# A gated recurrence beside full matmuls: products moved from GpSimd to VectorE, two scalings from VectorE to ScalarE

## The chip, the cores and the metric

The kernel runs on one core of one Trainium2 chip. The metric is the device time of one execution in microseconds, as the median of a few runs. The core has TensorE (PE, matmuls), VectorE (DVE), ScalarE (ACT), GpSimd (POOL) and SyncE (SP, which here only issues DMAs). Each engine works through its own instructions in a fixed order and waits where one of them needs a result of another engine.

## The reference, cut to what matters

One layer on 1024 prompt rows and 64 sample rows, 1024 wide (T = 1088 rows in all). The input is normed and projected; the columns of the projection are the recurrent branch's path `xa` and gate `ga`, the attention's q, k, v, and gates. Then, for the recurrent branch:

```python
ua, conv_new = causal_conv(xa, conv_hist, conv_w, conv_b)          # 4 taps: b + sum full[tap:tap+L] * w[tap]
r = sigmoid(einsum(ub, w_a) + b_a); i = sigmoid(einsum(ub, w_x) + b_x)
log_a = -LRU_C * r * softplus(-a_param)
a = exp(log_a); x_in = sqrt(-expm1(2 * log_a)) * (i * u)
h_t = a_t * h_{t-1} + x_t                                          # scan over the rows
ya = h * silu(ga)
```

Attention with forgetting runs beside it; both branches are projected, merged by sigmoid gates, projected again, normed and added.

## The kernel before, in words

The matmuls of this kernel reach fp32 precision by three passes: each operand is split into a high part (a copy on ScalarE, `wh`, `uh`, `yah`) and a low part (the difference on VectorE, `wl`, `ul`, `yal`), and `three` multiplies high by high, low by high and high by low. A weight panel is 1024 x 128; a panel against all rows takes 72 matmuls in three chunks of some 364 rows. `panel()` hands out a panel that is already split and at once splits the next one (ScalarE `wh`, L82, then VectorE `wl`, L85), into one of two buffers.

The stages are: norm and values (v); q, k and a few other panels by seven products of half-sized blocks for eight (`seven`, up to about 420 us), which `put` (L750) writes to DRAM; attention, with leftover panels between; the recurrence (about 862 to 1082 us); the two branch projections; the output projections.

In the products of halves `put` gets each half of a result from PSUM. Kind "r" (x's first panel, and the gate panels 1, 3 and 5 named by `GA_EARLY`) is stored as it is: a ScalarE copy or a VectorE add, and a DMA. The orders of ScalarE and VectorE are free in that stage.

In the recurrence the orders of TensorE, ScalarE and VectorE are the program's (L1466 and the manual schedule around it). Channels come in eight panels of 128, k = 0 to 7, and a tile holds 1092 columns: 1024 prompt rows, three of padding, 64 sample rows, and one more. Even and odd k have a set of tiles each (odd ones have names with `_e`), and each tile exists once, so the next even channel must wait until the last even one has been read. The steps for one k:

- `recur_in` (L1300): the gate weights' DMA, x's panel by TensorE, copied out by ScalarE into `xp`, one copy a chunk.
- `convolve` (L1332): the gate weights split (`g_h` on ScalarE, `g_l` on GpSimd), the first tap with its bias (L1339, VectorE), three more taps (L1342, VectorE) into `u`.
- `split_u` (L1346), `gate` (L1354): 18 matmuls, six sigmoids on ScalarE into `x` and `r`, then x times u (L1364) on GpSimd.
- `decay` (L1367): Exp and Tanh on ScalarE. `decay_a` (L1376): q, then 1-q (L1380), on VectorE. `root` (L1387): square root on ScalarE.
- `state_in` (L1391): two products on VectorE and one column copied by GpSimd. `scan` (L1398): VectorE's scan.
- `output` (L1410): the state times the gate's silu (L1420, L1421) on GpSimd, written over `sg` for even k. `split_y` (L1423): `yah`, `yal`.
- `own_gate` (L1428): the gate's panel, its sigmoid on ScalarE and product on VectorE chunk by chunk; for k = 1, 3, 5 a load of the stored panel, whose silu `early_gate` (L1443) takes in two instructions.

The loop (L1473) takes two channels a pass, k = 0, 2, 4, and a tail (L1512) the last two. Within a pass the steps of four channels are interleaved: `gate(k)` and `own_gate(k)`, `state` and `output` of k-1, x's panel of k+2, `gate(k+1)`, `convolve(k+2)`, then both decays, x's panel of k+3, both roots, `state(k)`. PSUM has eight banks in this stage.

Of the kernel before, what the change touches and what calls it, by code (L numbers as in the profile page):

```python
# [7 lines left out]
F32 = mybir.dt.float32  # L8
F32R = mybir.dt.float32r
AF = mybir.ActivationFunctionType  # L10
ALU = mybir.AluOpType
AX = mybir.AxisListType

P = 128
D = 1024
KT = D // P
SEQ = 1024
DEC = 64
T = SEQ + DEC
# [12 lines left out]
HT = T // 2  # L32
# [4 lines left out]
W_SC = 1092  # L37
# [28 lines left out]
def hybrid_step(tc, a, o):  # L66
    nc = tc.nc
    PSUM = bass.MemoryType.PSUM
    act, dve, pool, pe, sp = nc.scalar, nc.vector, nc.gpsimd, nc.tensor, nc.sync
# [8 lines left out]
    def f(ap):  # L78
        return ap.bitcast(F32)
# [4 lines left out]
    def sub(eng, out, in0, in1):  # L84
        return eng.tensor_tensor(out=out, in0=in0, in1=in1, op=ALU.subtract)  # L85
# [11 lines left out]
    d_x0 = dram.tile([P, T], F32, name="d_x0")  # L97
# [119 lines left out]
    quads = [([cols(c + p * P)], ((t, p), (t, p + 1))) for p in range(0, NP, 2) for c, t in ((C_K, "k"), (C_Q, "q"))]  # L217
    some = [(cols(C_XA, 1), d_x0)] + [(cols(C_GA + k * P, 1), d_ga[k]) for k in GA_EARLY]
    for (s1, d1), (s2, d2) in (some[:2], some[2:]):
        quads.append(([s1, s2], (("r", d1), ("r", d2))))  # L220
    for _ in range(MORE):
        src, (d1, d2) = gates.pop()
        quads.append(([src], (("r", d1), ("r", d2))))
# [387 lines left out]
    sp_ = sb("quad")  # L611
# [138 lines left out]
    def put(kind, arg, z, in1, h):  # L750

        s = kqp.tile([P, HT], F32, name="ko", tag="ko", bufs=4)
        s3 = s.rearrange("p (c n) -> p c n", c=2)
        if in1 is None:
            copy_act(s3, z)
        else:
            dve.tensor_tensor(out=s3, in0=z, in1=in1, op=ALU.add)
        if kind == "r":
            (act if in1 is None else sp).dma_start(arg[:, h * HT:(h + 1) * HT], s[:, :])
            return  # L760
        d = d_k if kind == "k" else d_q
        h_ = slice(h * HT, (h + 1) * HT)
        hi = sp_.tile([P, HT], F32R, name="oh", tag="oh", bufs=2)
        scale = 1.0 if kind == "k" else HD ** -0.5
        copy_act(hi[:, :], s[:, :], scale)
        act.dma_start(d[0, arg][:, h_], f(hi[:, :]))
        lo = sp_.tile([P, HT], F32, name="kl", tag="kl", bufs=1) if kind == "k" else s
        dve.scalar_tensor_tensor(out=lo[:, :], in0=s[:, :], scalar=scale, in1=f(hi[:, :]),
                                 op0=ALU.mult, op1=ALU.subtract)
        sp.dma_start(d[1, arg][:, h_], lo[:, :])  # L770
        if kind == "k":
            kept[arg, h] = s
            p = arg - arg % 2
            if (p, h) in kept and (p + 1, h) in kept:
                ss = [kept.pop((p + j, h)) for j in range(2)]
                c = 0
                for blocks in ((P, P), (P, P), (HT - 4 * P,)) if h == 0 else ((P, P), (P, SEQ - HT - 3 * P), (DEC,)):
                    owed.append((n_prod[0] + 1, lambda c=c, blocks=blocks: keys_out(p, ss, c, h * HT + c, blocks)))
                    c += sum(blocks)
# [510 lines left out]
    def cv(v, k):  # L1290
        return vt[:, v + k:v + k + 1]
# [3 lines left out]
    def room(name, k):  # L1295
        if k in lent_k:
            return lent[name][:, :]
        return p3.tile([P, T if name == "sg" else W_SC], F32, name=name)[:, :]
# [33 lines left out]
    def convolve(k):  # L1332
        xp, raw, gh, gl = xps.pop(k)
        copy_act(gh[:, :, :], raw[:, :, :])
        sub(pool, gl[:, :, :], raw[:, :, :], f(gh[:, :, :]))
        pool.tensor_copy(fin[:, 0:3, k], xp[:, SEQ:SEQ + 3])
        pool.tensor_copy(fin[:, 3:6, k], xp[:, W_SC - 1:W_SC + 2])
        u = room("u", k)
        dve.tensor_scalar(out=u, in0=xp[:, 0:W_SC], scalar1=cv(V_CW, k), scalar2=cv(V_CB, k),  # L1339
                          op0=ALU.mult, op1=ALU.add)  # L1340
        for tap in range(1, 4):
            dve.scalar_tensor_tensor(out=u, in0=xp[:, tap:tap + W_SC], scalar=cv(V_CW + tap * KT, k),  # L1342
                                     in1=u, op0=ALU.mult, op1=ALU.add)
        us[k], gws[k] = u, (gh, gl)
# [9 lines left out]
    def gate(k):  # L1354

        (u, uh, ul), (gh, gl) = us.pop(k), gws.pop(k)
        x, r = room("x", k), room("r", k)
        for i, dst, bias in ((1, x, V_BX), (0, r, V_BA)):
            for c in range(3):
                cs_ = slice(c * GC, (c + 1) * GC)  # L1360
                acc = mm.tile([P, 512], F32, name="gacc", tag="acc")
                three(acc[:, :GC], gh[:, i, :], gl[:, i, :], uh[:, cs_], ul[:, cs_], True, True)
                act.activation(out=dst[:, cs_], in_=acc[:, :GC], func=AF.Sigmoid, bias=cv(bias, k))
        (dve if k == KT - 1 else pool).tensor_tensor(out=x, in0=x, in1=u, op=ALU.mult)  # L1364
        sig[k] = x, r

    def decay(k):  # L1367

        x, r = sig[k]
        col = slice(k, k + 1)  # L1370
        e = room("e", k)
        act.activation(out=e, in_=r, func=AF.Exp, scale=nsp8[:, col])
        act.activation(out=r, in_=r, func=AF.Tanh, scale=sp4[:, col])
        eq[k] = e

    def decay_a(k):  # L1376
        e, t = eq[k], sig[k][1]
        q = room("q", k)
        dve.scalar_tensor_tensor(out=q, in0=e, scalar=1.0, in1=t, op0=ALU.add, op1=ALU.mult)
        dve.tensor_scalar(out=q, in0=q, scalar1=-1.0, scalar2=1.0, op0=ALU.mult, op1=ALU.add)  # L1380
        pool.memset(q[:, SEQ:SEQ + 3], 0.0)
        eq[k] = e, q

# [7 lines left out]
    def state_in(k):  # L1391
        (x, r), (e, q) = sig[k], eq[k]
        dve.scalar_tensor_tensor(out=r, in0=e, scalar=1.0, in1=r, op0=ALU.add, op1=ALU.mult)
        dve.tensor_tensor(out=x, in0=x, in1=r, op=ALU.mult)

        pool.tensor_copy(x[:, SEQ + 2:SEQ + 3], cv(V_H0, k))

    def scan(k):  # L1398
        col = slice(k, k + 1)
# [10 lines left out]
    def output(k):  # L1410
        sg, (r, e) = silus.pop(k), states.pop(k)
        if k == 5:
            y = p3.tile([P, W_SC + 3], F32, name="xp")[:, :W_SC]
        elif k == 7:
            y = room("r", 0)
        else:
            y = r if k in lent_k else sg
        outs[k] = y
        eng = dve if k == KT - 1 else pool
        eng.tensor_tensor(out=y[:, :SEQ], in0=e[:, :SEQ], in1=sg[:, :SEQ], op=ALU.mult)  # L1420
        eng.tensor_tensor(out=y[:, SEQ:T], in0=e[:, SEQ + 3:SEQ + 3 + DEC], in1=sg[:, SEQ:T], op=ALU.mult)  # L1421

    def split_y(k):  # L1423
        y = outs.pop(k)[:, :T]
        copy_act(ya[k][0][:, :T], y)
        sub(dve, ya[k][1][:, :T], y, f(ya[k][0][:, :T]))

    def own_gate(k):  # L1428
        sg = silus[k] = room("sg", k)

        def evac(c, t0, n, z):
            c_ = slice(t0, t0 + n)
            act.activation(out=sg[:, c_], in_=z, func=AF.Sigmoid)
            dve.tensor_tensor(out=sg[:, c_], in0=z, in1=sg[:, c_], op=ALU.mult)

        if k in GA_EARLY:
            sp.dma_start(sg[:, :T], d_ga[k])
            return None
        tag, w = panel()
        assert tag == ("g", k)  # L1440
        return panel_steps(mm, *w, xs, evac)

    def early_gate(k):  # L1443
        sg = silus[k]
        s = room("q", 0)
        act.activation(out=s[:, :T], in_=sg, func=AF.Sigmoid)
        dve.tensor_tensor(out=sg, in0=s[:, :T], in1=sg, op=ALU.mult)

    class Held:

# [21 lines left out]
    run(xa)  # L1472
    for k in range(0, KT - 2, 2):  # L1473
        gate(k)
        convolve(k + 1)
        if k:
            early_gate(k - 1)
        ga = own_gate(k)
        if k:
            split_y(k - 2)  # L1480
        chunk(ga)
        split_u(k + 1)
        chunk(ga)
        if k:
            state(k - 1)
            output(k - 1)
        run(ga)
        own_gate(k + 1)
        xa = recur_in(k + 2)
        chunk(xa)  # L1490
        chunk(xa)
        if k:
            split_y(k - 1)
        run(xa)
        gate(k + 1)
        convolve(k + 2)
        decay(k)
        xa = recur_in(k + 3)
        split_u(k + 2)
        decay_a(k)  # L1500
        chunk(xa)
        decay(k + 1)
        decay_a(k + 1)
        chunk(xa)
        root(k)
        root(k + 1)
        set_sigmoid()
        state(k)
        output(k)
        run(xa)  # L1510

    k = KT - 2  # L1512
    gate(k)
    convolve(k + 1)
    split_y(k - 2)
    split_u(k + 1)
    ga = own_gate(k)
    chunk(ga)
    chunk(ga)
    state(k - 1)  # L1520
    run(ga)
    early_gate(k - 1)
    output(k - 1)
    gate(k + 1)
    ga = own_gate(k + 1)
    decay(k)
    decay_a(k)
# [53 lines left out]
    for of in range(KT):  # L1581
        g = g_next
# [324 lines left out]
```

## Time and profile before

| | us |
|---|---|
| median of 3 runs (1490.17 to 1494.55) | 1492.96 |
| the profiled execution | 1493.34 |
| its span, first to last instruction | 1491.4 |
| TensorE busy | 1451.8 (97%) |
| VectorE busy | 884.6 (59%) |
| ScalarE busy | 689.6 (46%) |
| GpSimd busy | 367.9 (25%) |

A busy share is a mean over all stages. In the profile's rows a tile's name stands with an arrow to what it was computed from, `L` gives the line of the code, and a bracket at the end of a row of the timeline says how long the engine had been idle before it and what it waited for. The mean granted clock of TensorE is 0.988 of full speed.

### The profile page before, as it was taken

The numbers are of one execution on the slowest core, as the hardware profiler recorded it, in microseconds if no ns is written. First come the engines' busy times: TensorE is split into PE (matmuls) and PEld (weight loads), VectorE is DVE, ScalarE is ACT, GpSimd is POOL, SyncE is SP. The second block draws the span as 40 slices with busy tenths as digits, with TensorE's granted clock in tenths as the row PEclk, the third lists the DMA queues.
The fourth block names the chain that finished last, engine by engine and source line by source line (L and its number), as shares of the span: only waits on it lengthen the run. The fifth ranks groups of instructions, "written<-read, shape, count | busy, mean of one in ns | idle before, by whom it ended". The sixth has DMA issues, their size and how long they took to land.

```text
span 1491.4 us, 26313 instructions
## 1 busy us (share of the span) xinstructions
PE 1451.8 (97%) x10096; PEld 1427.3 (96%) x10096; DVE 884.6 (59%) x1516; ACT 689.6 (46%) x1327; POOL 367.9 (25%) x443
## 2 busy tenths in 40 slices
PE   7999999999999999999999999989999999999997
PEld 7999999999999999999899999988999999999997
DVE  5464765664326666666556556999755545337644
ACT  4423444442225566565555536556544323334633
POOL 3012332322322333233233223555322000000001
PEclk9999999999999999999999999999999999999999
DMA  5367455753375756555753331211276544215111
GB/s 201 107 128 102 144 164 172 192 182 101 105 199 147 135 130 154 116 134 131 135 133 95 59 86 38 55 42 39 88 254 237 197 135 140 86 34 170 47 47 43
DMA packets 141081, 182.84 MB, mean 123 GB/s; under 512 B 23164, under 2 KB 111708, under 8 KB 140956
## 3 DMA queue, kind: packets, MB, share of 16 engines
q1 hardware_dynamic: 123292, 155.53, 40.2%
q10 hardware_dynamic: 17664, 25.64, 4.9%
q8 instruction: 79, 1.29, 0.3%
q14 instruction: 46, 0.38, 0.1%
HBM read 122.65 MB, written 58.46 MB: 121 GB/s over the span
## 4 chain that ended last, share of the span: by engine, by line
PE 80%; DVE 8%; ACT 5%; DMA 3%; issue 2%; POOL 1%; SPq 0%; ACTq 0%; DVEq 0%; POOLq 0%
PE quad L726 16%; PE acc L160 13%; PE acc L158 13%; PE acc L159 13%; PE tp L1068 4%; PE pv L1096 3%; PE pv L1098 2%; PE s L1046 2%; PE s L1047 2%; PE vacc L158 1%; PE vacc L159 1%; PE vacc L160 1%; DVE u L1342 1%; DMA out_v_prompt<-v_sb 1%; PE vacc L456 1%
## 5 line engine op out<-in xcount | busy, mean ns | idle before, releaser
L160 PE MATMUL acc<-xh,wl 128*128 128x364 f32 (+1 forms) x768 | 253.4, 330 | 6.8 <-DVE wl L85 6.8
L158 PE MATMUL acc<-xh,wh 128*128 128x364 f32 (+1 forms) x768 | 254.3, 331 | 0.4 <-ACT st L82 0.4
L159 PE MATMUL acc<-xl,wh 128*128 128x364 f32 (+1 forms) x768 | 253.0, 329 | 0.0
L160 PEld LDWEIGHTS acc<-xh,wl 128*128 128x128 f32 x768 | 145.5, 189 | 7.4 <-DVE wl L85 7.4
L158 PEld LDWEIGHTS acc<-xh,wh 128*128 128x128 f32 x768 | 146.0, 190 | 1.4 <-ACT st L82 0.7
L159 PEld LDWEIGHTS acc<-xl,wh 128*128 128x128 f32 x768 | 145.7, 190 | 0.6
L85 DVE TENSOR_TENSOR wl<-w_raw,wh 128x1024 fp32r<-128x1024 f32 (+1 forms) x66 | 84.7, 1285 | 56.5 <-ACT wh L82 55.6
L1031 POOL TENSOR_SCALAR pb<-pb,sm 128x896 f32<-128x896 f32 (+1 forms) x64 | 61.7, 964 | 203.5 <-DVE sm L1030 184.0
L1026 DVE CUSTOM_DVE_ANT_0 s<-s,mask 128x1024 f32<-128x1024 f32 (+7 forms) x128 | 95.4, 767 | 25.5 <-PE s L1047 25.2
L82 ACT ACTIVATE wh<-w_raw 128x1024 fp32r<-128x1024 f32 (+1 forms) x66 | 64.4, 977 | 60.9 <-PE quad L726 27.5
L85 DVE TENSOR_TENSOR tl<-tp,th 128x512 fp32r<-128x512 f32 x96 | 65.8, 689 | 36.9 <-ACT th L82 36.8
L726 PE MATMUL quad<-xh,wh 128*128 128x272 f32 x384 | 80.7, 291 | 0.0
L726 PE MATMUL quad<-xl,wh 128*128 128x272 f32 x384 | 79.5, 288 | 0.0
L726 PE MATMUL quad<-xh,wl 128*128 128x272 f32 x384 | 79.4, 288 | 0.0
L1028 ACT ACTIVATE pb<-s,nm 128x896 f32<-128x896 f32 (+1 forms) x64 | 61.2, 955 | 33.9 <-DVE nm L1026 25.0
L82 ACT ACTIVATE th<-tp 128x512 fp32r<-128x512 f32 x96 | 57.0, 597 | 41.0 <-PE tp L1068 37.0
L158 PE MATMUL acc<-wqh,hth 128*128 128x256 f32 x256 | 73.0, 285 | 0.0
L158 PE MATMUL acc<-wqh,mxh 128*128 128x256 f32 x256 | 72.5, 283 | 0.0
L159 PE MATMUL acc<-wql,mxh 128*128 128x256 f32 x256 | 72.4, 283 | 0.0
L160 PE MATMUL acc<-wqh,mxl 128*128 128x256 f32 x256 | 72.4, 283 | 0.0
L159 PE MATMUL acc<-wql,hth 128*128 128x256 f32 x256 | 72.4, 283 | 0.0
L160 PE MATMUL acc<-wqh,htl 128*128 128x256 f32 x256 | 72.4, 283 | 0.0
(535 smaller groups left out, 4274.6 us busy)
## 6 DMA issues: line engine op xcount, KB each, us to landing
w_raw<-in_w_in SPq DMA_DIRECT2D x60, 256.0 KB
q<-d_q SPq DMA_DIRECT2D x48, 256.0 KB
k<-d_k SPq DMA_DIRECT2D x48, 256.0 KB
w_raw<-in_w_branch SPq DMA_DIRECT2D x32, 256.0 KB
w_raw<-in_w_in SPq DMA_DIRECT2D x56, 128.0 KB
wraw<-in_w_in SPq DMA_DIRECT2D x20, 256.0 KB
d_k<-oh ACTq DMA_DIRECT2D x16, 272.0 KB
d_k<-kl SPq DMA_DIRECT2D x16, 272.0 KB
```

Of the source, the lines that this page charges most:

```text
L82: return act.activation(out=out, in_=in_, func=AF.Copy, scale=scale)
L85: return eng.tensor_tensor(out=out, in0=in0, in1=in1, op=ALU.subtract)
L158: pe.matmul(out, ah, bh, start=start, stop=False)
L159: pe.matmul(out, ah, bl, start=False, stop=False)
L160: pe.matmul(out, al, bh, start=False, stop=stop)
L726: pe.matmul(acc[:, c, :CW], l[:, k, :], r[:, k, c * CW:(c + 1) * CW], start=(first and k == 0 and p == 0), stop=(k == 3 and p == 2), skip_ ...
L1026: at = book("D", now[0] + HOP_PE, per(D_MAX, n), lambda: dve.tensor_tensor_reduce(out=s[:, :n], in0=s[:, :n], in1=m, scale=-1.0, scalar=-N ...
L1028: free = book("A", at, per(A_EXP, n), lambda: act.activation(out=pr[:, :n], in_=s[:, :n], func=AF.Exp, scale=-1.0, bias=nm, accum_out=sm))
L1031: return free, book("G", at, per(G_NORM, n), lambda: pool.tensor_scalar(out=pr[:, :n], in0=pr[:, :n], scalar1=sm, scalar2=1.0, op0=ALU.mul ...
L1046: pe.matmul(s[:, c0:c0 + w], t["q1"][:, q0:q0 + P], t["k1"][:, c0:c0 + w], start=True, stop=False)
L1068: pe.transpose(tp[:, o0 + i * P:o0 + (i + 1) * P], pr[par][:, kb * P:(kb + 1) * P], ident[:, :])
L1096: pe.matmul(pv[:, :256], v, tl[:, c], start=(g == 0 and j == 0), stop=False)
```

## The change

- The three early gate panels become kind "g": `put` takes their silu before it stores them (a sigmoid on ScalarE, a product on VectorE, half by half). `early_gate` is gone, and `own_gate` loads a finished silu.
- In `convolve` the gate weights' low part goes from GpSimd to VectorE, and the first tap with its bias from VectorE to ScalarE.
- x times u goes from GpSimd to VectorE and becomes a step of its own, `gated`, which is called after the next `convolve`.
- `decay_a`: 1-q goes from VectorE to ScalarE.
- `state_in`: the copied column goes from GpSimd to VectorE. `output`: both products go from GpSimd to VectorE.
- In the loop and the tail `own_gate(k)` is called before `convolve(k+1)`, so its panel split stands ahead of the taps.

```diff
-        quads.append(([s1, s2], (("r", d1), ("r", d2))))
+        quads.append(([s1, s2], (("r" if d1 is d_x0 else "g", d1), ("g", d2))))
...
-        if kind == "r":
+        if kind == "g":
+            sg = sp_.tile([P, HT], F32, name="kl", tag="kl", bufs=1)
+            act.activation(out=sg[:, :], in_=s[:, :], func=AF.Sigmoid)
+            dve.tensor_tensor(out=s[:, :], in0=s[:, :], in1=sg[:, :], op=ALU.mult)
+        if kind in "rg":
             (act if in1 is None else sp).dma_start(arg[:, h * HT:(h + 1) * HT], s[:, :])
             return
...
     def convolve(k):
         copy_act(gh[:, :, :], raw[:, :, :])
-        sub(pool, gl[:, :, :], raw[:, :, :], f(gh[:, :, :]))
+        sub(dve, gl[:, :, :], raw[:, :, :], f(gh[:, :, :]))
...
-        dve.tensor_scalar(out=u, in0=xp[:, 0:W_SC], scalar1=cv(V_CW, k), scalar2=cv(V_CB, k),
-                          op0=ALU.mult, op1=ALU.add)
+        act.activation(out=u, in_=xp[:, 0:W_SC], func=AF.Identity, scale=cv(V_CW, k), bias=cv(V_CB, k))
...
-        (dve if k == KT - 1 else pool).tensor_tensor(out=x, in0=x, in1=u, op=ALU.mult)
+        sig[k] = x, r, u
+
+    def gated(k):
+        x, r, u = sig[k]
+        dve.tensor_tensor(out=x, in0=x, in1=u, op=ALU.mult)
         sig[k] = x, r
...
     def decay_a(k):
         dve.scalar_tensor_tensor(out=q, in0=e, scalar=1.0, in1=t, op0=ALU.add, op1=ALU.mult)
-        dve.tensor_scalar(out=q, in0=q, scalar1=-1.0, scalar2=1.0, op0=ALU.mult, op1=ALU.add)
+        act.activation(out=q, in_=q, func=AF.Copy, scale=-1.0, bias=1.0)
         pool.memset(q[:, SEQ:SEQ + 3], 0.0)
...
-        pool.tensor_copy(x[:, SEQ + 2:SEQ + 3], cv(V_H0, k))
+        dve.tensor_copy(x[:, SEQ + 2:SEQ + 3], cv(V_H0, k))
...
-        eng = dve if k == KT - 1 else pool
-        eng.tensor_tensor(out=y[:, :SEQ], in0=e[:, :SEQ], in1=sg[:, :SEQ], op=ALU.mult)
-        eng.tensor_tensor(out=y[:, SEQ:T], in0=e[:, SEQ + 3:SEQ + 3 + DEC], in1=sg[:, SEQ:T], op=ALU.mult)
+        dve.tensor_tensor(out=y[:, :SEQ], in0=e[:, :SEQ], in1=sg[:, :SEQ], op=ALU.mult)
+        dve.tensor_tensor(out=y[:, SEQ:T], in0=e[:, SEQ + 3:SEQ + 3 + DEC], in1=sg[:, SEQ:T], op=ALU.mult)
...
     for k in range(0, KT - 2, 2):
         gate(k)
+        ga = own_gate(k)
         convolve(k + 1)
-        if k:
-            early_gate(k - 1)
-        ga = own_gate(k)
+        gated(k)
         if k:
             split_y(k - 2)
...
         gate(k + 1)
         convolve(k + 2)
+        gated(k + 1)
         decay(k)
...
     k = KT - 2
     gate(k)
+    ga = own_gate(k)
     convolve(k + 1)
+    gated(k)
     split_y(k - 2)
     split_u(k + 1)
-    ga = own_gate(k)
...
     run(ga)
-    early_gate(k - 1)
     output(k - 1)
     gate(k + 1)
+    gated(k + 1)
     ga = own_gate(k + 1)
```

More of the change, by code (lines that the diff above doesn't have):

```diff
@@ L1441, in own_gate @@
         return panel_steps(mm, *w, xs, evac)
[L1443 to L1447, printed above, removed]
     class Held:
```

## The prediction, made before the result was known

> **What bounds the kernel now.** First the page: the span and the busy times.
>
> ```profile
> span 1491.4 us, 26313 instructions
> ...
> PE 1451.8 (97%) x10096; PEld 1427.3 (96%) x10096; DVE 884.6 (59%) x1516; ACT 689.6 (46%) x1327; POOL 367.9 (25%) x443
> ```
>
> TensorE is busy but for 39.6 us, so nothing can win more than some of that. Next, what TensorE waited for from 860 to 1100 us, the recurrence (total, times, longest), and the busy times in one pass of its loop, from the end of scan(0) to the end of scan(2), beside 20 us in which TensorE never waits.
>
> ```profile
> PE acc L160 <- DVE wl L85: 7.2, 3, 4.3
> PE gacc L159 <- DVE ul L85: 4.3, 2, 3.7
> ```
>
> ```profile
> 929.47:977.31 47.84, 45.28 (x264) 44.98 (x263) 44.23 (x31) 29.00 (x43) 25.86 (x28) 0.96 0.19 48
> 1100.00:1120.00 20.00, 20.00 (x124) 20.00 (x123) 9.09 (x11) 8.12 (x8) 3.36 (x2) 1.00 0.80 258
> ```
>
> The columns are length, then PE, PEld, DVE, ACT, POOL busy. A pass gives TensorE 252 matmuls (three panels of 72, two gates of 18): at 124 in 20 us that is 40.6 us. It takes 47.84, and VectorE is busy for 44.23 of it: VectorE sets the pace, and the stalls are late VectorE results. 7.2 us a pass could be won.
>
> Now the order of work in that pass, which both engines keep: ScalarE, then VectorE (start, duration, tile).
>
> ```profile
> 956.82 1.48 ACT L1363 ACTIVATE x_e<-gacc,vt 128x364 f32<-128x364 f32 x3
> ...
> 959.50 0.47 ACT L82 ACTIVATE g_h<-st 128x256 fp32r<-128x256 f32 x1
> 959.99 1.28 ACT L1372 ACT_TABLE_LOAD   x1
> 961.28 1.22 ACT L1372 ACTIVATE e<-r,nsp 128x1092 f32<-128x1092 f32 x1
> 962.53 1.21 ACT L1373 ACTIVATE r<-r,sp 128x1092 f32<-128x1092 f32 x1
> 963.65 1.05 ACT L82 ACTIVATE wh<-w_raw 128x1024 fp32r<-128x1024 f32 x1
> 965.33 1.12 ACT L82 ACTIVATE uh<-u 128x1092 fp32r<-128x1092 f32 x1 [0.64 <-DVE u L1342]
> 966.36 0.46 ACT L82 ACTIVATE xp<-acc 128x364 f32<-128x364 f32 x1
> ...
> 970.82 1.12 ACT L1389 ACTIVATE r<-r 128x1092 f32<-128x1092 f32 x1
> ```
>
> ```profile
> 927.04 2.43 DVE L1401 TENSOR_TENSOR_SCAN e<-q,x 128x1092 f32<-128x1092 f32 x1 [0.29 <-POOL x L1396]
> ...
> 949.00 2.43 DVE L1401 TENSOR_TENSOR_SCAN e_e<-q_e,x_e 128x1092 f32<-128x1092 f32 x1 [0.28 <-POOL x_e L1396]
> 951.35 0.51 DVE L1434 TENSOR_TENSOR sg<-acc,sg 128x360 f32<-128x360 f32 x1
> 951.77 3.44 DVE L85 TENSOR_TENSOR wl<-w_raw,wh 128x1024 fp32r<-128x1024 f32 x1
> 956.55 1.29 DVE L85 TENSOR_TENSOR yal<-r_e,yah 128x1088 fp32r<-128x1088 f32 x1 [1.34 <-ACT yah L82]
> 957.75 0.84 DVE L1339 TENSOR_SCALAR u<-xp,vt 128x1092 f32<-128x1092 f32 x1
> 958.63 6.66 DVE L1342 SCALAR_TENSOR_TENSOR u<-xp,vt,u 128x1092 f32<-128x1092 f32 x3
> 965.22 1.22 DVE L85 TENSOR_TENSOR wl<-w_raw,wh 128x1024 fp32r<-128x1024 f32 x1
> 966.49 1.30 DVE L85 TENSOR_TENSOR ul<-u,uh 128x1092 fp32r<-128x1092 f32 x1
> 967.70 1.29 DVE L1379 SCALAR_TENSOR_TENSOR q<-e,r 128x1092 f32<-128x1092 f32 x1
> 969.02 0.73 DVE L1380 TENSOR_SCALAR q<-q 128x1092 f32<-128x1092 f32 x1
> ...
> 971.97 1.30 DVE L1393 SCALAR_TENSOR_TENSOR r<-e,r 128x1092 f32<-128x1092 f32 x1 [0.25 <-ACT r L1389]
> ...
> 974.88 2.43 DVE L1401 TENSOR_TENSOR_SCAN e<-q,x 128x1092 f32<-128x1092 f32 x1 [0.28 <-POOL x L1396]
> ```
>
> The reader is to see two things. VectorE rows are stretched where GpSimd works (wl takes 3.44 us once, 1.22 us the other time). And from u ready (965.29) to r (971.97) ScalarE alone runs in series, while VectorE does wl, ul and both q with their 1-a beside it and is done just in time (0.25 us of waiting).
>
> **The change part by part.** GpSimd's products cost this where they go; rows of both engines:
>
> ```profile
> L1342 DVE SCALAR_TENSOR_TENSOR u_e<-xp,vt,u_e x12: 1355/1356/3619, 880.3 to 1030.7; 128x1092 f32<-128x1092 f32 x12
> L1364 POOL TENSOR_TENSOR x_e<-x_e,u_e x3: 2548/2560/3132, 911.2 to 1006.2; 128x1092 f32<-128x1092 f32 x3
> L1420 DVE TENSOR_TENSOR r<-e_e,sg_e x1: 1225/1225/1225, 1072.5 to 1072.5; 128x1024 f32<-128x1024 f32 x1
> L1421 DVE TENSOR_TENSOR r<-e_e,sg_e x1: 218/218/218, 1073.7 to 1073.7; 128x64 f32<-128x64 f32 x1
> ```
>
> On VectorE a gated product takes 1.30 us (like ul), an output 1.23+0.22=1.45, and the low part of the gate weights 0.42 (an estimate from the last two rows: 1.05 ns an element between 64 and 1024). Without GpSimd a tap takes 1.36 instead of up to 3.62. VectorE's work in a pass: for each of two channels 0.42+4.07+1.30 (ul)+1.30+1.29+1.30+1.30+2.43+1.45+1.29 = 16.15, with three wl and three sg 37.5 us, against 44.23. By SBUF — State Buffer, section Who interferes with whom, of the Trainium skill, a VectorE instruction with two SBUF inputs and a GpSimd instruction that reads SBUF lock each other out for the whole instruction. By that rule the trace agrees (1.36 against 3.62 us), and it speaks for the change.
>
> ScalarE gets two first taps and two 1-a in a pass and loses half of the early silus. No row has Identity with two pointers: between uh (1.12) and Exp with a pointer (1.22), I take 1.2; it could gain 0.1 by overlap, or lose a table load (below). 1-a is the form of uh: 1.1. ScalarE's sum rises to some 32.5 us. Neither engine is full; but both run in a fixed order, so what counts is who waits for whom. I walk the pass; T0 is the end of scan(k).
>
> *T0 to the end of scan(k+1).* Before: 949.00+2.43-929.47 = 21.96. After: own_gate now stands before convolve, so behind output(k) VectorE's next is wl, which waits for ScalarE: six sigmoids (956.82 to 959.50, 2.7; they wait for the scan, as before) and wh 1.05. Then wl 1.2, gl 0.4, three taps 4.1, gated 1.3, yal 1.25; sg on ScalarE 0.45 (its tile is free only then), uh 1.05, ul 1.3, sg 0.45, r 1.3, x 1.35, the copy and the scan 2.6: 20.5 us. The wl stall of TensorE goes: wl is ready at T0+5 instead of T0+12. Gain 1.5.
>
> *To u(k+2) ready.* Before 965.29-951.43 = 13.86. After: output 1.45, yah 1.1, xp 0.5, six sigmoids 2.7, gh 0.45, first tap 1.2, three taps 4.1: 11.5. Gain 2.4. VectorE's sg, wl and yal lie beside ScalarE's part; VectorE is idle for some 2.7 us before the taps, since the first tap is queued behind the sigmoids.
>
> *To r.* Before 6.68. After, 1-a(k) on ScalarE waits for q, which VectorE reaches after gated 1.3, wl 1.2, ul 1.25 and q 1.3 (5.05; uh lies beside). Behind it in ScalarE's queue stand xp, Exp and Tanh of k+1; VectorE's q(k+1) waits for Tanh; ScalarE's 1-a(k+1) waits for that; the square roots stand behind that. So 5.05 + 1.1 + 0.45 + 1.2 + 1.2 + q 1.3 + 1.1 + 0.45 + table 1.3 + root 1.1 = 14.25, all in series. Loss 7.6. TensorE waits here for banks, since x's three sums are read later.
>
> *To the end of scan(k+2).* 5.34 before, 5.25 after: GpSimd's one-column copy goes.
>
> Sum 51.5 against 47.84: +3.65 a pass, two passes (k=2 and 4): +7.3. For the first pass and the tail:
>
> ```profile
> 909.01 0.53 ACT L82 ACTIVATE xp<-acc 128x296 f32<-128x296 f32 x2 [3.52 <-PE acc L160]
> ```
>
> ```profile
> 924.13 1.30 DVE L1393 SCALAR_TENSOR_TENSOR r<-e,r 128x1092 f32<-128x1092 f32 x1
> ...
> 1022.71 2.43 DVE L1401 TENSOR_TENSOR_SCAN e<-q,x 128x1092 f32<-128x1092 f32 x1 [0.29 <-POOL x L1396]
> ...
> 1058.03 1.30 DVE L1393 SCALAR_TENSOR_TENSOR r<-e,r 128x1092 f32<-128x1092 f32 x1 [0.19 <-ACT r L1389]
> ...
> 1064.60 2.66 DVE L1393 SCALAR_TENSOR_TENSOR r_e<-e_e,r_e 128x1092 f32<-128x1092 f32 x1
> ...
> 1075.13 1.29 DVE L85 TENSOR_TENSOR yal<-r,yah 128x1088 fp32r<-128x1088 f32 x1
> ```
>
> In k=0 TensorE sets the pace until x(2)'s last copy (909.54); from there to r was 14.59. After: sigmoids 2.9, gh 0.45, first tap 1.2, taps 4.1, then the 14.25: 22.9, +8.3. Convolve(0), for which TensorE stands still, has its first tap at 1.2 instead of 0.84: +0.4. The tail from 1025.14 to r(6) was 32.9; after: 19.4 to the end of scan(5) (the walk above less 1.1, sg being beside uh), then sigmoids 2.7, wh 1.05, table 1.3, Exp 1.2, Tanh 1.2, q 1.3, 1-a 1.1, Exp 1.2, Tanh 1.2, q 1.3, 1-a 1.1, wh 1.05, table 1.3, root 1.1: 37.5, +4.6. From r(6) to the last yal nothing: output(6) costs VectorE 1.45 and r_e beside it (2.66) goes back to 1.30.
>
> The early silus: six halves of a sigmoid and a product, under
>
> ```profile
> 360.00:380.00 20.00, 20.00 (x161) 20.00 (x161) 8.48 (x11) 5.14 (x8) 5.90 (x4) 1.00 0.22 73
> ```
>
> where both engines idle more than half: nothing. Without that cover at most 6 x 1.35 and two table loads, 10.7. The stores on SP's queue leave 1.35 later; the tiles are read 500 us on. SP's loads of early gates wait for output(k+1), which is earlier.
>
> Sum: 0.4+8.3+7.3+4.6 = 20.6. The profiled execution took 1493.34, 0.4 above the median 1492.96: 1513.5 us.
>
> **The rivals.** *VectorE's load decides (faster).* If what sets a pass is busy time, 37.5 and 32.5 us lie under TensorE's 40.6, and two passes win 7.2 each: 1479. For it: 44.23 of 47.84 before, and the stretched rows. The lock that the Trainium skill states (SBUF — State Buffer, Who interferes with whom) is this rival's rule: with GpSimd's reads gone VectorE would have its stretch back. Against it: the fixed order. It decides if the way from u to r grows by less than the 3.9 that the first two parts win.
> *No change:* it grows by just that in the passes and the first pass is hidden: 1493.
> *Identity needs a table:* 1.28 twice in a pass on the path, once in the first and in the tail: 7.7 more, 1521. Against: Copy (uh, xp) runs among Exp and Sqrt without a load of its own. ScalarE: Activation LUTs, section Table sets: the hidden batching unit, of the Trainium skill has identity as filler in every set; no run here shows it yet.
> *The silus stall the products:* up to 10.7 more, 1524.
>
> **How the numbers follow.** Forecast 0.78, load decides 0.12, no change 0.03, table 0.05, silus 0.02. The walk's steps overlap by up to 0.1 each and leave out hand-overs of as much: with half of the wait for wl or the tap gone in each pass it is 1503, with the table 1522. A change under 0.3% (4.5 us) can't be told from none. Slower 0.85, same 0.03, faster 0.12.
>
> **What would show it.** Right: ScalarE waiting some 3.6 us for q in front of each first 1-a, VectorE 4 us for Tanh and 4 us for the root; scans of even channels 51.5 us apart; taps all near 1.36. Wrong: passes near 41 us with TensorE full; table loads at convolve; TensorE waits in the products.

## The result: slower by 1.3%, and the profile after

The changed kernel takes 1513.25 us (median of 4 runs, 1511.96 to 1515.3) against 1493.28 for the kernel before in the same sessions: a ratio of 1.013, with a 95% interval from 1.0112 to 1.0148. The forecast was 1513.5, in a range from 1503 to 1522.

The page of the changed kernel, the lines that answer to those shown of before:

```profile
span 1510.3 us, 26329 instructions
...
PE 1457.5 (97%) x10096; PEld 1430.3 (95%) x10096; DVE 864.7 (57%) x1540; ACT 709.8 (47%) x1348; POOL 309.3 (20%) x406
```

VectorE has become 20 us less busy (884.6 before) although it took over GpSimd's products, and the time is 20 us longer. So work is not what decides. TensorE's waits of the changed kernel from 860 to 1100 us, the window of the view before (total, times, longest):

```profile
PE acc L158 <- ACT xp L82: 11.2, 3, 4.4
PE gacc L158 <- ACT uh L82: 7.3, 2, 5.0
...
PE acc L160 <- DVE wl L85: 0.7, 2, 0.5
```

The wait for wl is down from 7.2 to 0.7 us, as the walk in the prediction had it. In its place TensorE waits for ScalarE to copy x's sums out of the banks, and longer for uh (7.3 us, against 1.9 before). One pass of the loop, from the end of scan(0) to the end of scan(2) (length, then PE, PEld, DVE, ACT, POOL busy):

```profile
937.16:988.37 51.21, 44.46 (x254) 43.06 (x253) 36.55 (x35) 32.19 (x46) 9.73 (x18) 0.97 0.18 45
```

51.21 us instead of 47.84, while VectorE's work fell from 44.23 to 36.55 and GpSimd's from 25.86 to 9.73. Two more rows of the changed kernel show why VectorE's work fell, and what a tap on ScalarE costs (shortest, median and longest in ns):

```profile
L1345 DVE SCALAR_TENSOR_TENSOR u_e<-xp,vt,u_e x12: 1354/1356/1360, 887.8 to 1048.0; 128x1092 f32<-128x1092 f32 x12
...
L1343 ACT ACTIVATE u<-xp,vt x4: 1293/1304/1310, 872.2 to 1015.1; 128x1092 f32<-128x1092 f32 x4
```

No tap is stretched any more (the longest was 3619). Now the pass itself in the changed kernel's timeline, ScalarE first and then VectorE (start, duration, tile, and in brackets the idle time before):

```profile
969.59 1.10 ACT L82 ACTIVATE uh<-u 128x1092 fp32r<-128x1092 f32 x1
973.92 1.12 ACT L1387 ACTIVATE q<-q 128x1092 f32<-128x1092 f32 x1 [3.23 <-DVE q L1386]
974.94 0.46 ACT L82 ACTIVATE xp<-acc 128x364 f32<-128x364 f32 x1
975.29 1.20 ACT L1379 ACTIVATE e_e<-r_e,nsp 128x1092 f32<-128x1092 f32 x1
976.52 1.21 ACT L1380 ACTIVATE r_e<-r_e,sp 128x1092 f32<-128x1092 f32 x1
979.09 1.11 ACT L1387 ACTIVATE q_e<-q_e 128x1092 f32<-128x1092 f32 x1 [1.36 <-DVE q_e L1386]
980.11 0.46 ACT L82 ACTIVATE xp<-acc 128x364 f32<-128x364 f32 x1
980.58 1.28 ACT L1396 ACT_TABLE_LOAD   x1
981.87 1.11 ACT L1396 ACTIVATE r<-r 128x1092 f32<-128x1092 f32 x1
```

```profile
934.73 2.43 DVE L1408 TENSOR_TENSOR_SCAN e<-q,x 128x1092 f32<-128x1092 f32 x1
...
941.07 1.22 DVE L85 TENSOR_TENSOR wl<-w_raw,wh 128x1024 fp32r<-128x1024 f32 x1 [2.52 <-ACT wh L82]
...
955.29 2.43 DVE L1408 TENSOR_TENSOR_SCAN e_e<-q_e,x_e 128x1092 f32<-128x1092 f32 x1
...
963.80 0.43 DVE L85 TENSOR_TENSOR g_l<-st,g_h 128x256 fp32r<-128x256 f32 x1 [1.90 <-ACT g_h L82]
964.99 4.14 DVE L1345 SCALAR_TENSOR_TENSOR u<-xp,vt,u 128x1092 f32<-128x1092 f32 x3 [0.77 <-ACT u L1343]
969.05 1.29 DVE L1371 TENSOR_TENSOR x_e<-x_e,u_e 128x1092 f32<-128x1092 f32 x1
...
972.60 1.29 DVE L1386 SCALAR_TENSOR_TENSOR q<-e,r 128x1092 f32<-128x1092 f32 x1
977.76 1.29 DVE L1386 SCALAR_TENSOR_TENSOR q_e<-e_e,r_e 128x1092 f32<-128x1092 f32 x1 [3.88 <-ACT r_e L1380]
983.02 1.30 DVE L1400 SCALAR_TENSOR_TENSOR r<-e,r 128x1092 f32<-128x1092 f32 x1 [3.97 <-ACT r L1396]
...
985.94 2.43 DVE L1408 TENSOR_TENSOR_SCAN e<-q,x 128x1092 f32<-128x1092 f32 x1
```

Read the brackets in order of time. ScalarE waits 3.23 us for q; VectorE then waits 3.88 us for Tanh, ScalarE 1.36 us for q_e, VectorE 3.97 us for the root. While the one engine works the other stands: they hand one line of work to and fro. In the kernel before, once uh had its u, the only wait in that stretch was VectorE's 0.25 us for the root. The rows that bound the first pass and the tail, in the changed kernel:

```profile
908.69 0.53 ACT L82 ACTIVATE xp<-acc 128x296 f32<-128x296 f32 x2 [3.52 <-PE acc L160]
```

```profile
931.81 1.29 DVE L1400 SCALAR_TENSOR_TENSOR r<-e,r 128x1092 f32<-128x1092 f32 x1 [3.97 <-ACT r L1396]
...
1037.41 2.43 DVE L1408 TENSOR_TENSOR_SCAN e<-q,x 128x1092 f32<-128x1092 f32 x1
...
1077.49 1.29 DVE L1400 SCALAR_TENSOR_TENSOR r<-e,r 128x1092 f32<-128x1092 f32 x1 [1.20 <-ACT r L1396]
...
1094.46 1.29 DVE L85 TENSOR_TENSOR yal<-r,yah 128x1088 fp32r<-128x1088 f32 x1
```

From the end of x(2)'s last copy to the end of the last yal the stage takes 186.53 us (1095.75-909.22) against 166.88 before (1076.42-909.54): 19.65 us more. The two profiled spans differ by 18.9 us and the medians by 19.97, so no other stage has to be searched.

### The profile page after: what moved, and what is told of

It reads as the page before. It is cut to its first block, busy times and chain, and to the rows that moved or that the text cites. A ratio compares the mean times of both kernels' runs of the same rounds, so it can differ in the third digit from the quotient of the medians.

```text
span 1510.3 us, 26329 instructions
## 1 busy us (share of the span) xinstructions
PE 1457.5 (97%) x10096; PEld 1430.3 (95%) x10096; DVE 864.7 (57%) x1540; ACT 709.8 (47%) x1348; POOL 309.3 (20%) x406
## 4 chain that ended last, share of the span: by engine, by line
PE 80%; DVE 8%; ACT 5%; DMA 4%; issue 2%; SPq 0%; POOL 0%; ACTq 0%; DVEq 0%; POOLq 0%
PE quad L726 16%; PE acc L158 13%; PE acc L160 13%; PE acc L159 13%; PE tp L1072 4%; PE pv L1100 3%; PE pv L1102 2%; PE s L1050 2%; PE s L1051 2%; PE vacc L158 1%; PE vacc L159 1%; PE vacc L160 1%; DVE u L1345 1%; PE vacc L456 1%; DMA q<-d_q 1%
## 5 line engine op out<-in xcount | busy, mean ns | idle before, releaser
L85 DVE TENSOR_TENSOR wl<-w_raw,wh 128x1024 fp32r<-128x1024 f32 (+1 forms) x66 | 75.8, 1150 | 74.8 <-ACT wh L82 73.2
L82 ACT ACTIVATE th<-tp 128x512 fp32r<-128x512 f32 x96 | 56.9, 596 | 40.6 <-PE tp L1072 36.6
```

The lines of the kernel that those rows point to most:

```text
L82: return act.activation(out=out, in_=in_, func=AF.Copy, scale=scale)
```

## The experiments

The theory, called the series theory: on ScalarE, 1-a stands in a queue ahead of the copies, Exp, Tanh and roots of the next channel, and makes one line out of what ran side by side. The rivals: the tap and the new place of own_gate cost the time; ScalarE's added work costs it; VectorE's busy time decides. The times below are medians, and each ratio is against the kernel before in the same session.

**1. 1-a back on VectorE.** In the changed kernel:

```diff
-        act.activation(out=q, in_=q, func=AF.Copy, scale=-1.0, bias=1.0)
+        dve.tensor_scalar(out=q, in0=q, scalar1=-1.0, scalar2=1.0, op0=ALU.mult, op1=ALU.add)
```

> The changed kernel with 1-a alone back on VectorE. Series theory (ScalarE's 1-a makes the way from u to r one line): from u ready VectorE does gated 1.3, wl 1.2, ul 1.25, q 1.3, 1-a 0.7 while ScalarE runs uh, xp, Exp, Tanh, xp, table load, root without waiting; r(k) starts 6.4 us earlier in each of the three passes and r(6) 4.9 us earlier in the tail: 1513.3-24.1 = 1489, scans of even channels 44.8 us apart. Theory that the tap's and own_gate's new places cost the time: VectorE gets 0.7 more twice a pass and nothing else changes: 1513 to 1517.

Measured 1489.86 us, ratio 0.9974 (0.996 to 0.9989). A pass of this kernel, and its r row:

```profile
933.10:977.82 44.72, 44.19 (x266) 43.57 (x265) 37.84 (x37) 30.06 (x44) 7.56 (x18) 1.00 0.21 52
```

```profile
972.49 1.29 DVE L1400 SCALAR_TENSOR_TENSOR r<-e,r 128x1092 f32<-128x1092 f32 x1
```

VectorE does 1.3 us more work in a pass and the pass is 6.5 us shorter; r waits for nothing. One line of the change carries more than its whole loss: the rest of it wins some 4 us.

**2. The first tap back on VectorE.** In the changed kernel:

```diff
-        act.activation(out=u, in_=xp[:, 0:W_SC], func=AF.Identity, scale=cv(V_CW, k), bias=cv(V_CB, k))
+        dve.tensor_scalar(out=u, in0=xp[:, 0:W_SC], scalar1=cv(V_CW, k), scalar2=cv(V_CB, k),
+                          op0=ALU.mult, op1=ALU.add)
```

> The changed kernel with the first tap alone back on VectorE (the low part of the gate weights stays ahead of it). Series theory: the taps behind the sigmoids start as before, since VectorE still waits there for g_h; the taps of the odd channels end 0.85 later: 1513.3 + 2.9 = 1516 (1514 to 1517). Theory that the tap on ScalarE costs the time: the 2 to 3 us that VectorE waits ahead of the even taps go in each pass: 1503.

Measured 1516.73 us, ratio 1.0149 (1.0134 to 1.0164), so the tap's place does not explain the loss. The even taps of this kernel:

```profile
967.44 0.43 DVE L85 TENSOR_TENSOR g_l<-st,g_h 128x256 fp32r<-128x256 f32 x1 [1.90 <-ACT g_h L82]
967.78 1.03 DVE L1343 TENSOR_SCALAR u<-xp,vt 128x1092 f32<-128x1092 f32 x1
968.86 4.14 DVE L1346 SCALAR_TENSOR_TENSOR u<-xp,vt,u 128x1092 f32<-128x1092 f32 x3
```

VectorE waits the same 1.90 us for g_h, since g_l stands ahead of the taps in its order. Before the taps on ScalarE it waited another 0.77 us for the first tap; on VectorE that tap takes 1.03 us itself, so its engine makes little difference here.

**3. 1-a alone, in the kernel before.**

```diff
-        dve.tensor_scalar(out=q, in0=q, scalar1=-1.0, scalar2=1.0, op0=ALU.mult, op1=ALU.add)
+        act.activation(out=q, in_=q, func=AF.Copy, scale=-1.0, bias=1.0)
```

> The kernel before with 1-a alone moved to ScalarE. Series theory: u to r becomes wl 1.2, ul 1.25, q 1.3, 1-a 1.1, xp 0.45, Exp 1.2, Tanh 1.2, q 1.3, 1-a 1.1, xp 0.45, table 1.3, root 1.1 = 12.95 instead of 6.7, +6.2 in each of three passes, +5 in the tail: 1493.3 + 23.7 = 1517, slower than the whole change. Load theory (busy VectorE decides): VectorE is relieved of 1.5 us a pass, 1488 to 1493.

Measured 1515.42 us, ratio 1.015 (1.013 to 1.0169). ScalarE of this kernel, and a pass:

```profile
974.83 1.12 ACT L1380 ACTIVATE q<-q 128x1092 f32<-128x1092 f32 x1 [2.57 <-DVE q L1379]
...
980.00 1.11 ACT L1380 ACTIVATE q_e<-q_e 128x1092 f32<-128x1092 f32 x1 [1.36 <-DVE q_e L1379]
```

```profile
935.35:989.28 53.93, 45.58 (x253) 44.98 (x252) 42.78 (x29) 31.21 (x45) 25.82 (x28) 0.91 0.18 43
```

The same waits, with none of the other edits. A pass takes 53.93 us (47.84 and the forecast 6.2 make 54.0), though VectorE is busy for 1.45 us less. Within the whole change the same line costs some 23 us (experiment 1), alone 21.

**4. 1-a stays on ScalarE, behind the roots.** Of the changed kernel's `decay_a` the part after q becomes `one_minus`:

```diff
         root(k)
         root(k + 1)
+        one_minus(k)
+        one_minus(k + 1)
         set_sigmoid()
```

> The changed kernel with 1-a left on ScalarE, but both of them issued behind both roots (the scan is the first to need them). Series theory: it is the place in the queue and not ScalarE's work that costs; r(k) starts when the root is done, 6.6 us earlier in each pass, 5.0 in the tail, and 1-a is done before the scan: 1513.3-24.9 = 1488, scans 44.6 us apart. Theory that ScalarE's added work costs the time: no change, 1513.

Measured 1490.64 us, ratio 0.9974 (0.9962 to 0.9986). ScalarE and VectorE of this kernel:

```profile
970.12 1.12 ACT L1399 ACTIVATE r<-r 128x1092 f32<-128x1092 f32 x1
971.14 1.10 ACT L1399 ACTIVATE r_e<-r_e 128x1092 f32<-128x1092 f32 x1
972.15 1.10 ACT L1391 ACTIVATE q<-q 128x1092 f32<-128x1092 f32 x1
973.16 1.10 ACT L1391 ACTIVATE q_e<-q_e 128x1092 f32<-128x1092 f32 x1
```

```profile
971.27 1.30 DVE L1403 SCALAR_TENSOR_TENSOR r<-e,r 128x1092 f32<-128x1092 f32 x1 [1.11 <-ACT r L1399]
...
974.19 2.43 DVE L1411 TENSOR_TENSOR_SCAN e<-q,x 128x1092 f32<-128x1092 f32 x1
```

ScalarE does the same work as in the changed kernel, in another order, and the 23 us are gone. 1-a(k) ends at 973.25, before the scan that reads it. So neither ScalarE's load nor the hand-over as such costs the time, but what stands behind it in the queue.

**5. The taps ahead.** Kernel 4, with the first tap back on VectorE and `convolve` cut in two, `taps` (the four taps) and `split_g` (the gate weights):

```diff
         gate(k)
+        taps(k + 1)
         ga = own_gate(k)
-        convolve(k + 1)
+        split_g(k + 1)
         gated(k)
...
         gate(k + 1)
-        convolve(k + 2)
+        taps(k + 2)
+        split_g(k + 2)
         gated(k + 1)
```

> The kernel with 1-a behind both roots, and besides the first tap back on VectorE and the taps issued ahead of the gate weights' low part and ahead of own_gate. Series theory: what is left of a pass (44.5) is a line too, and the two places where VectorE stood idle ahead of the taps (2.5 us for wh, 2.7 us for sigmoids, g_h and tap) go for 0.85 each: the pass comes to some 41.9, the first pass wins 1.2, the tail 1.5: 1490.6-8 = 1482 (1479 to 1486), TensorE's 40.6 a pass being close. Load theory (VectorE's busy time decides): VectorE gets 1.7 us more a pass, 1490 to 1495.

Measured 1478.96 us, ratio 0.9904 (0.988 to 0.9928): faster than both kernels. Its pass:

```profile
931.56:973.30 41.74, 41.74 (x254) 41.74 (x253) 38.06 (x37) 30.08 (x44) 7.08 (x18) 1.00 0.23 55
```

By these rows TensorE never stops in it, so little is left to win in a pass. The pass is 41.74 us (forecast 41.9). The 40.6 us that the prediction worked out for 252 matmuls, from 20 us of another stage, is thus about 1.1 too small for this one. Which of the two edits, the tap's engine or the order, wins how much was not taken apart.

**6. The products back on GpSimd.** Kernel 1, with x times u and the outputs as they were before:

```diff
-        dve.tensor_tensor(out=x, in0=x, in1=u, op=ALU.mult)
+        (dve if k == KT - 1 else pool).tensor_tensor(out=x, in0=x, in1=u, op=ALU.mult)
...
-        dve.tensor_tensor(out=y[:, :SEQ], in0=e[:, :SEQ], in1=sg[:, :SEQ], op=ALU.mult)
-        dve.tensor_tensor(out=y[:, SEQ:T], in0=e[:, SEQ + 3:SEQ + 3 + DEC], in1=sg[:, SEQ:T], op=ALU.mult)
+        eng = dve if k == KT - 1 else pool
+        eng.tensor_tensor(out=y[:, :SEQ], in0=e[:, :SEQ], in1=sg[:, :SEQ], op=ALU.mult)
+        eng.tensor_tensor(out=y[:, SEQ:T], in0=e[:, SEQ + 3:SEQ + 3 + DEC], in1=sg[:, SEQ:T], op=ALU.mult)
```

> The changed kernel with 1-a back on VectorE, and with x times u and the outputs back on GpSimd. Lock theory: VectorE is relieved of 5.5 us a pass but each of four GpSimd products stretches a VectorE neighbour by about 2.2 us, and yah waits for the slower output: a pass 1 to 3 us longer than 44.7, 1492 to 1499. Plain load theory: VectorE's 5.5 us less a pass shorten it, TensorE's 40.6 decides: 1478 to 1483.

Measured 1495.64 us, ratio 1.0017 (1.0 to 1.0034), 5.8 us above kernel 1 (medians of two sessions). Its pass and the most stretched row of VectorE:

```profile
930.16:977.20 47.04, 44.81 (x269) 43.97 (x268) 37.37 (x30) 30.03 (x44) 17.70 (x24) 1.00 0.20 49
```

```profile
951.21 3.45 DVE L85 TENSOR_TENSOR wl<-w_raw,wh 128x1024 fp32r<-128x1024 f32 x1
```

VectorE gave away 5.5 us of products and its busy time fell by 0.47 only (37.84 to 37.37): its other rows are longer by some 4.5 us in all. The expectation had 2.2 us for each of the four products; the rows show 2.23 (the wl above, 1.22 without a product beside it), 1.45 (the wl at 934.08) and 0.78 (the g_l at 959.45), and nothing for the fourth product, beside which VectorE stands idle.

The pass is 2.3 us longer, but not by these rows. The whole of it lies between the end of scan(k+1) and u(k+2), which takes 13.92 us here and 11.42 in kernel 1; the other three steps together are 0.2 shorter. ScalarE's yah waits there for the output, and the six sigmoids stand behind it in the queue; first kernel 1, then this one:

```profile
955.10 1.12 ACT L82 ACTIVATE yah<-r_e 128x1088 fp32r<-128x1088 f32 x1 [5.75 <-DVE r_e L1427]
```

```profile
954.85 1.11 ACT L82 ACTIVATE yah<-r_e 128x1088 fp32r<-128x1088 f32 x1 [8.15 <-POOL r_e L1428]
```

yah starts 1.44 us after the end of the scan in kernel 1 and 3.98 after it here, since the output takes GpSimd 2.40 and 1.28 us and VectorE 1.23 and 0.22. So what the pass gains from this part of the change is the output's shorter time on the line of work; the stretched rows mostly lie beside the line. Moving these products off GpSimd is worth 2.3 us a pass, and it is the part of the change that helps.

**7. The early silus alone, in the kernel before.** The edit of `put` and the calls of `early_gate` taken out, as in the change:

```diff
-        if k:
-            early_gate(k - 1)
```

> The kernel before with only the early silus moved among the products of halves. Series theory with idle cover in the products: VectorE loses its product (3.6 us stretched, of which the next row inherits some 2) in two passes and 1.3 in the tail, nothing is paid among the products: 1493.7-4 to -8 = 1486 to 1490. If the products' stage pays for them: up to 10 us more, 1494 to 1500.

Measured 1492.93 us, ratio 1.0002 (0.9986 to 1.0017): not to be told from none, where 4 to 8 us had been expected. Its pass and the rows after the taps:

```profile
931.20:977.89 46.69, 45.84 (x276) 45.14 (x275) 43.06 (x30) 27.88 (x42) 25.90 (x28) 1.00 0.20 49
```

```profile
938.07 3.56 DVE L85 TENSOR_TENSOR wl<-w_raw,wh 128x1024 fp32r<-128x1024 f32 x1
941.55 1.82 DVE L85 TENSOR_TENSOR yal<-sg,yah 128x1088 fp32r<-128x1088 f32 x1
```

In the kernel before, the same place has:

```profile
936.36 3.62 DVE L1447 TENSOR_TENSOR sg_e<-q,sg_e 128x1088 f32<-128x1088 f32 x1
939.90 1.74 DVE L85 TENSOR_TENSOR wl<-w_raw,wh 128x1024 fp32r<-128x1024 f32 x1
941.56 1.28 DVE L85 TENSOR_TENSOR yal<-sg,yah 128x1088 fp32r<-128x1088 f32 x1
```

The silu's product (3.62 us) had been one of the stretched rows. With it gone wl stands next to GpSimd's product and takes 3.56 us instead of 1.74, and yal 1.82 instead of 1.28, so a pass wins 1.15 us and not 3.6. From x(2)'s last copy to the last yal the stage is 2.0 us shorter, less than the medians can tell. The products of halves paid nothing: 40 us of that stage, before and with the whole change,

```profile
340.00:380.00 40.00, 40.00 (x321) 40.00 (x320) 16.22 (x21) 10.27 (x16) 11.82 (x8) 1.00 0.31 83
```

```profile
340.00:380.00 40.00, 40.00 (x321) 40.00 (x320) 23.74 (x28) 15.35 (x23) 11.88 (x8) 1.00 0.29 77
```

hold the same 321 matmuls, with VectorE 7.5 and ScalarE 5.1 us busier.

## Why the prediction was right, point by point

| step | forecast | measured |
|---|---|---|
| T0 to the end of scan(k+1) | 20.5 | 20.56 |
| to u(k+2) ready | 11.5 | 11.41 |
| to r | 14.25 | 13.89 |
| to the end of scan(k+2) | 5.25 | 5.35 |
| a pass, against 47.84 | 51.5 | 51.21 and 51.47 |
| first pass, x(2) to r, against 14.59 | 22.9 | 22.59 |
| tail to r(6), against 32.89 | 37.5 | 37.65 |
| r(6) to the last yal, start to start, against 17.10 | same | 16.97 |
| convolve(0) | +0.4 | +0.39, not in the total |
| early silus among the products | 0 | 0 |

The measured column is from the rows above: for instance 955.29+2.43-(934.73+2.43) = 20.56, and 983.02-(964.99+4.14) = 13.89. The sum of the differences is 8.0+3.4+3.6+4.8-0.1 = 19.7 against the forecast 20.6. The 0.9 too much lies mainly in two places. Each way to r is about 0.3 shorter than forecast, where steps of ScalarE overlap by about 0.1; in the pass of k = 4 the first step, 20.83, takes that back. And convolve(0) cost its 0.4 (from the start of wh to u(0) 13.15 us instead of 12.76) without passing it on: from the same start to the end of x(2)'s last copy the changed kernel takes 44.71 us and the one before 45.29. One duration was too small: the first tap takes 1.30 us and not 1.2.

The signs that the prediction named came too: ScalarE waits 3.23 us for q (3.6 forecast), VectorE 3.88 and 3.97 (4 each), the even scans are 51.21 and 51.47 apart, and no tap is above 1.36. So the mechanism was right, term by term. That the time itself was met within 0.3 us is partly luck: the terms miss by 0.3 to 0.4 in both directions, and the runs of one kernel differ by 3 to 4 us.

The rival on the other side, that VectorE's load decides, had its premises right (36.55 us of work in a pass, all stretch gone) and its conclusion wrong; experiments 1, 3 and 4 each tell it apart. Its condition was the right one: the way from u to r must grow by less than what the rest wins. It grew by 7.2 against 3.85. In experiment 1 it grows by 0.7 (7.41 against 6.68), and the time is below the kernel before. In experiment 5 the time is the 1479 of that rival, but partly by chance: two passes win 6.1 each and not 7.2, and 1.6 comes from the tail. The table rival is out: no ACT_TABLE_LOAD stands at L1343. That is what the Trainium skill states (ScalarE: Activation LUTs, Table sets: the hidden batching unit, identity is in every set), and here the trace agrees. The lock (SBUF — State Buffer, Who interferes with whom, of the Trainium skill) is borne out by the taps' 1360 ns at most after the change, and by experiment 6, where wl takes 3.45 us beside a GpSimd product and 1.22 without one.

What the prediction did not price is which part of the change wins what. The silus were worth less than their own stretched rows say (experiment 7): GpSimd's product stretched the next row instead.

## What to carry to other kernels

Before a short step is moved to a less busy engine with a fixed order, read what stands behind it in that engine's queue, and walk both queues: one 1.1 us instruction that waits for the other engine cost 6 us a pass and 21 us in all (experiment 3), while both engines were busy for a smaller share of the pass. The same instruction cost next to nothing behind the roots, where only the scan still had to wait for it: place it behind everything that others wait for sooner. A GpSimd product is not priced by GpSimd's idle time, but by two things: its own longer time where others wait for it (an output of 3.7 us instead of 1.45 made a pass 2.3 us longer), and the stretch of the VectorE rows beside it (0 to 2.2 us each in experiment 6), which costs time only where those rows are waited for.

## What the runs showed of the hardware that was not expected

An ACTIVATE over 1092 columns takes 1.12 us with immediates (1-a), 1.21 with one pointer operand (Exp, Tanh) and 1.30 with two (the first tap): 0.09 us a pointer. The Trainium skill (ScalarE: Activation LUTs, What ACT_TABLE_LOAD costs) gives about 93 ns for each; the trace agrees.

Stretch moves on: taking a stretched VectorE row away (the silu's product, 3.62 us in the pass) won 1.15 us there, since the next row was stretched instead (wl, 3.56 instead of 1.74 us).
